# A two-layer diffusion trunk on one core: where the modulation loads and the attention stacks are queued, what landing times the planner assumes, and new strand ranks

## The chip, the cores and the metric

One core of one Trainium2 chip. The metric is the device time of one execution in microseconds, as the median of several runs. Work on the core is done by TensorE (PE, matrix products), VectorE (DVE), ScalarE (ACT), GpSimd (POOL) and by DMA transfers that SyncE (SP), ACT and POOL issue, each in the order of its own queue.

## The reference

Two layers over 512 latent tokens and 256 context tokens, 1024 wide. Cut to what matters:

```python
sh1, sc1, gt1, sh2, sc2, gt2 = split(silu(c) @ w_ada + b_ada, 6)     # latents; the context likewise with c_ctx
h = rmsnorm(x, g1) * (1 + sc1) + sh1
z = h @ w_in                                                       # nine groups of 256 columns
q, k = rope(z[q]), rope(z[k]);  k_all, v_all = context ++ latents
a = softmax(q1 k1) - lam * softmax(q2 k2);  o = a @ v_all          # 4 heads, differential attention
mix = concat(mixer_a(z), mixer_b(z), mixer_c(z), rmsnorm(o))
x = x + gt1 * (mix @ w_out)
h2 = rmsnorm(x, g2) * (1 + sc2) + sh2
x = x + gt2 * ((silu(dwconv3(h2 @ up_a)) * (h2 @ up_b)) @ w_down)   # D_FF = 2816
# the context tokens run through the same weights in layer 0; the second layer needs only their keys and values
return rmsnorm(x, final_g)
```

All is float32. A product is made in three passes: each operand is split into a rounded part (`hi`, `wh`) and the rest (`lo`, `wl`), and PE adds hi*wh, lo*wh and hi*wl.

## The kernel before

The kernel writes no fixed order. It is a set of generators ("strands") that ask for operations, and a planner (`Sched`) that keeps a modelled time for each engine, for each tile's last write and read, and for the DMA system. At each step it advances the strand whose next operation could start first by that model; among those that could start now, the one with the lowest rank (`prio`) goes first. So every constant of the model (`SPC`, the cost of an issue on SP; `LAT`, the latency of a queue) and every rank (`PMC`, `PATT`, `PGM`, `PLATER`, ...) decides in which order instructions are put on the engines' queues. On the chip each queue then runs in that order, and an instruction that waits holds all that stand behind it.

The stages that the steps below speak of:

- **Start.** `start` loads the eight tiles of x, then two "pairs" of modulation weights (`load_pair`, three DMAs of `w_ada0` each, into slots of the pool S), then starts `load_units`, which streams all other weights through SP in the order of `plan`; after three weights it waits until all eight first pairs are issued. `ada_pair` multiplies a pair on PE, transposes the row and adds the bias, which gives one block of shift and scale; `make_h` then makes the block's normed input: `ht` (DVE), `hhi` (ACT), `hlo` (DVE). The first three projections (`batch_t` with q, k and the gate input) go through the eight blocks as these come.
- **Later pairs.** `later` loads and multiplies twelve more pairs, one after the other, for the rest of layer 0's modulation.
- **Stacks.** For attention the rotated q and k are copied to the layout that the score products need: `make_stacks` and `stack` issue 64 SBUF-to-SBUF DMAs per layer, each of 32 partitions, on SP or POOL, as the planner finds earlier.
- **Norm in the middle of a layer.** `final_pass` makes the output projection for one group of tokens after the other and sums squares; `after_mid` makes the normed input `h2`, and stores x to `xacc` in DRAM. The feed-forward products with halves combined (`quads`) need the whole numbers of `h2`: `right_factors` adds `hhi` and `hlo` on POOL (`b`, 8 per layer) and forms the sums `t` from them.
- **Feed-forward.** PE streams w_up and w_dn; ACT rounds each weight (`wh`), DVE or POOL makes the rest (`wl`, `wl_engine`); ACT evicts the down products (`ev`), which POOL's DMAs add to `xacc` in DRAM.
- **Modulation of layer 1.** `next_ada` and `ada_blocks` work through 56 blocks of `w_adaT` (512 KB each) while layer 0's feed-forward and layer 1's beginning run: one DMA on SP, then one or two multiply-and-sum instructions of 128x1024 on DVE, then the bias. They have two buffers of their own. One strand does load and sum in turn.
- **Norm between the layers.** `final_pass` and `after_last` of layer 0 make layer 1's input, and `state["norm"]` is set from the second group on until it is done.

The flag `state["attention"]` limits the engine of `wl` while attention runs: POOL, if its modelled time is less than `WLA` ahead of DVE's.

Of the kernel before, what the change touches and what calls it, by code (L numbers as in the profile page):

```python
# [9 lines left out]
F32 = mybir.dt.float32  # L10
# [70 lines left out]
class Sched:  # L81
# [10 lines left out]
    def __init__(self, nc):  # L92
        self.nc = nc
        self.T = dict(pe=0.0, act=0.0, dve=0.0, pool=0.0, sp=0.0)
        self.dclk = 0.0
        self.port = 0.0
        self.now = 0.0
        self.busy = {}
        self.strands = []
        self.W, self.R = {}, {}  # L100
        self.table = None
        self.full = False
        self.count = 0

# [24 lines left out]
    def _ready(self, req):  # L129
        if callable(req):  # L130
            return req()
        opts, outs, ins, lock = req
        t = [(max(self._deps(o[0], outs, ins) + (PEM if o[0] == "pe" else 0.0), self.T[o[0]],
                  self.port if o[0] in lock else 0.0), o[1]) for o in opts]
        return min(t, key=lambda v: v[0] + v[1])[0] if RDY else min(t)[0]

# [52 lines left out]

    def dma(self, out, in_, queues=("sp",), as_=None):  # L190

        nc = self.nc
        eng = dict(sp=nc.sync, act=nc.scalar, pool=nc.gpsimd)
        cost = dict(sp=SPC, act=0.41, pool=0.55)
        sb = [ap for ap in (out, in_) if ap.space != bass.MemoryType.DRAM]
        outs = [out] if out.space != bass.MemoryType.DRAM else []
        ins = [in_] if in_.space != bass.MemoryType.DRAM else []
        n = 1
        for d in sb[0].shape:
            n *= d  # L200
        t0 = dict(self.T)
        yield from self.op([(q, cost[q], lambda q=q: eng[q].dma_start(*(as_ or (out, in_)))) for q in queues], outs, ins)  # L202
        e = next(q for q in queues if self.T[q] != t0[q])
        self.dclk = max(self.dclk, self.T[e]) + 4 * n / self.BW / 1e3
        t = self.dclk + self.LAT[e]
        for o in outs:
            self._note(self.W, o, t, "dma")
        for i in ins:
            self.R[i.tensor.name].append((*span(i)[1:], t, "dma"))
# [232 lines left out]
def build(tc, a, out):  # L442
    nc = tc.nc
    es = ExitStack()
    with es:
# [9 lines left out]
        K = Sched(nc)  # L455
# [200 lines left out]

        def ada_blocks(l, js, nv, AR, silu, junk):

            for j in js:
                w = yield from AR.get("adaw")  # L660
                yield from K.dma(w, a["w_adaT"][l, j])
                if l and ADAG:
# [27 lines left out]
        def load_pair(b, keep=0):  # L690
            raw = []
            for i in range(3):
                n = 768 if i < 2 else 512
                w = yield from S.get("adaw", keep=keep)
                yield from K.dma(w[:, 0:n], a["w_ada0"][b, i][:, 0:n])
                raw.append(w)
# [163 lines left out]
        def stack(hl, order, r):  # L860
            st = yield from S.get("stk", F32R, keep=KA)
            w = hl[2]
            if STK2:
                for o in range(2):
                    src = hl[o][32 * r:32 * r + 32, 0:w].bitcast(F32)
                    if order[1]:
                        whole, at = st[:, 0:w], st[:, 0:w].rearrange("(a b p) w -> b p a w", a=2, b=2)[o]
                    else:
                        whole = st[64 * o:64 * o + 64, 0:w]
                        at = whole.rearrange("(a p) w -> p a w", a=2)  # L870
                    yield from K.dma(whole.bitcast(F32), src, STKQ, (at.bitcast(F32), src.unsqueeze(1).to_broadcast([32, 2, w])))
                return st
            for i, o in enumerate(order):
# [353 lines left out]
        def start():  # L1227
# [19 lines left out]
            for j in range(2 if START == 0 else 1, 8):  # L1247
                yield from K.when(lambda: j < state.get("blocks", 0) + 5)
                raw0[j] = yield from load_pair(j)
            state["pairs"] = 8  # L1250

        def start_consts():
# [69 lines left out]
        def layer(l):  # L1322
# [44 lines left out]
            K.spawn(bx_copy(pp[2], T, xs, 0), 1)  # L1367
            K.spawn(make_stacks(res, stk), 1)
            if l == 0:
                yield from second_q()  # L1370
                K.spawn(lambdas(), 1)
            if l == 0:
                def later():
                    for i in range(12):
                        raw = yield from load_pair(8 + i, KM)
                        yield from ada_pair(raw, (16 + 2 * i, 17 + 2 * i), 1)
                    yield from make_a(0, 1)
                K.spawn(later(), PLATER)

            def tok_group(g, toks_list, post):  # L1380
# [153 lines left out]
            if not last:  # L1534
                def next_ada():
# [5 lines left out]
                    junk = pool.tile([128, 1024], F32, tag="junk", name="junk")  # L1541
                    AR = Slots(K, pool, [128, 1024], "ar", 2, bufs=2)
                    yield from K.dma(silu, a["cc"], ("pool",))
# [275 lines left out]
QUADS = (0, 1)  # L1819
SPC = 0.36  # L1820
BACT = False
PRF = (1, 1)
MB0 = 3
AVALL = True
SWC = 0.09
RDY = False
PB = 1
LAZY = False
START = 0
STK2 = False  # L1830
EARLY = True
RLQ = ('pool',)
ADAG = 0
PLAIN = (4, 6)
# [5 lines left out]
WLP = 1  # L1840
WLA = 1
WLU = 10
MB = 4
PMC = (1.6, 0.9)
PATT = (1, 0.8)
PATV = (0.9, 1)
PGM = (0.8, 1)
PCMB = (1.1, 1.1)
STKQ = ('sp', 'pool')
KEEP = 1  # L1850
NAQ = 5
KM = 4
KA = 2
NX = 5
PLATER = 1.8
NWR = 4
# [118 lines left out]
```

## Time and profile before

| | us |
|---|---|
| median of 3 runs (1481.15 to 1483.77) | 1482.09 |
| the profiled execution | 1487.35 |
| its span | 1485.5 |
| PE busy in the span | 1425.6 (96%) |
| DVE busy | 1118.8 (75%) |
| ACT busy | 743.2 (50%) |
| POOL busy | 294.0 (20%) |

The span is the time between the first and the last instruction of the profiled execution; 1.9 us of its time lie around it. Busy times are sums over instructions of the profile; PE's granted clock is 0.983 of full speed in the mean.

### The profile page before, as it was taken

Reading aid. Unit: us, or ns where it says so; the run is one execution under the profiler, and the core shown is the slowest. Engines: PE = TensorE matmul, PEld = TensorE weight load, DVE = VectorE, ACT = ScalarE, POOL = GpSimd, SP = SyncE. Lnnn points to the kernel's source line nnn. Section 1 sums busy time; section 2 is a strip of 40 time slices with the busy share of each in tenths; the row PEclk is TensorE's granted clock in tenths of the full one; section 3 lists DMA queues with packets and bytes.
Section 4 is the critical chain, followed back from the end, with each engine's and each line's share of the span. In section 5 each row is a group of like instructions: output and inputs, shape, how many; then the busy total and the mean of one; then the engine's idle time right before and its main releaser. Section 6 shows DMA issues by size and latency. Waiting matters only on the chain.

```text
span 1485.5 us, 23946 instructions
## 1 busy us (share of the span) xinstructions
PE 1425.6 (96%) x9196; PEld 1269.7 (85%) x9196; DVE 1118.8 (75%) x1912; ACT 743.2 (50%) x1185; POOL 294.0 (20%) x320
## 2 busy tenths in 40 slices
PE   6989999999899999999999898999999999999997
PEld 3866888897799999999999886888888889999996
DVE  4727578767788778888777778698878758777875
ACT  5325646524443455545545433465545455665652
POOL 0200232213200021101111110343413011221130
PEclk8989999999999999999999999999999999999998
DMA  9475241324015687667977844524332366677661
GB/s 373 141 236 201 89 132 43 128 86 157 15 59 165 163 210 166 172 169 189 226 191 196 270 170 151 171 100 135 118 108 73 122 134 157 162 181 184 177 191 58
DMA packets 76835, 229.13 MB, mean 154 GB/s; under 512 B 10624, under 2 KB 12800, under 8 KB 76592
## 3 DMA queue, kind: packets, MB, share of 16 engines
q1 hardware_dynamic: 50832, 160.34, 31.7%
q0 software_dynamic: 25600, 66.86, 21.3%
q8 instruction: 72, 1.18, 0.3%
q10 hardware_dynamic: 288, 0.39, 0.1%
q14 instruction: 43, 0.35, 0.1%
HBM read 164.64 MB, written 51.38 MB: 145 GB/s over the span
## 4 chain that ended last, share of the span: by engine, by line
PE 86%; DVE 6%; DMA 4%; SPq 1%; issue 1%; ACT 1%; DVEq 0%; ACTq 0%
PE banks L231 84%; DMA adaw<-in_w_ada 2%; PE banks L244 2%; DMA adaw<-in_w_adaT 1%; SPq L202 1%; DVE wl L283 1%; DVE hlo L299 1%; DVE ht L299 1%; DVE fy L299 0%; ACT hhi L263 0%; DMA mats<-in_mats 0%; DVE by L299 0%; DVE out L299 0%; DVE u L283 0%; DVE ropey L283 0%
## 5 line engine op out<-in xcount | busy, mean ns | idle before, releaser
L273 ACT CAST wh<-wr 128x1024 fp32r<-128x1024 f32 x220 | 229.6, 1048 | 172.1 <-PE banks L231 129.1
L231 PE MATMUL banks<-hlo,wh 128*128 128x512 f32 (+2 forms) x968 | 300.0, 334 | 8.3 <-DVE hlo L299 8.2
L231 PE MATMUL banks<-hhi,wh 128*128 128x512 f32 (+2 forms) x968 | 302.1, 336 | 4.7 <-DVE fy L299 2.1
L231 PE MATMUL banks<-hhi,wl 128*128 128x512 f32 (+2 forms) x968 | 298.6, 333 | 0.4 <-DVE wl L283 0.4
L283 DVE TENSOR_TENSOR wl<-wr,wh 128x1024 fp32r<-128x1024 f32 x196 | 240.2, 1227 | 73.1 <-ACT wh L273 72.6
L213 POOL DMA_DIRECT2D xacc<-ev x128 | 110.8, 866 | 602.7 <-ACT ev L312 590.0
L231 PEld LDWEIGHTS banks<-hlo,wh 128*128 128x128 f32 x968 | 173.5, 190 | 26.9 <-DVE hlo L299 13.9
L231 PEld LDWEIGHTS banks<-hhi,wh 128*128 128x128 f32 x968 | 173.6, 190 | 22.1 <-issue 2.6
L231 PEld LDWEIGHTS banks<-hhi,wl 128*128 128x128 f32 x968 | 173.3, 189 | 14.6 <-DVE wl L283 0.6
L231 PE MATMUL banks<-hi,wh 128*128 128x512 f32 (+1 forms) x560 | 172.0, 349 | 4.2 <-ACT hi L273 4.2
L231 PE MATMUL banks<-lo,wh 128*128 128x512 f32 (+1 forms) x560 | 171.2, 348 | 2.8 <-DVE lo L283 2.6
L231 PE MATMUL banks<-hi,wl 128*128 128x512 f32 (+1 forms) x560 | 170.7, 347 | 0.0
L312 ACT ACTIVATE ev<-banks,ada 128x512 f32<-128x512 f32 x192 | 111.2, 614 | 76.6 <-PE banks L231 51.3
L231 PEld LDWEIGHTS banks<-hi,wh 128*128 128x128 f32 x560 | 96.3, 189 | 18.2 <-ACT hi L273 4.8
L231 PEld LDWEIGHTS banks<-lo,wh 128*128 128x128 f32 x560 | 96.2, 189 | 17.2 <-DVE lo L283 3.5
L231 PEld LDWEIGHTS banks<-hi,wl 128*128 128x128 f32 x560 | 95.9, 189 | 14.3
L283 DVE TENSOR_TENSOR wr<-wr 128x512 f32<-128x512 f32 x136 | 91.0, 687 | 17.3 <-DMA wr<-in_w_up 16.2
L285 POOL TENSOR_TENSOR wl<-wr,wh 128x1024 fp32r<-128x1024 f32 (+1 forms) x24 | 58.8, 2448 | 210.1 <-ACT wh L273 154.7
L231 PE MATMUL banks<-th,wh 128*128 128x384 f32 (+1 forms) x272 | 84.4, 310 | 0.4 <-DVE c L283 0.4
L231 PE MATMUL banks<-th,wl 128*128 128x384 f32 (+1 forms) x272 | 84.5, 311 | 0.0
L231 PE MATMUL banks<-tl,wh 128*128 128x384 f32 (+1 forms) x272 | 84.4, 310 | 0.0
L325 DVE TENSOR_REDUCE mx<-banks 128x1 f32<-128x768 f32 (+1 forms) x80 | 67.7, 847 | 17.8 <-PE banks L231 16.7
(234 smaller groups left out, 2958.2 us busy)
## 6 DMA issues: line engine op xcount, KB each, us to landing
wr<-in_w_up SPq DMA_DIRECT2D x88, 512.0 KB, 4.6
adaw<-in_w_adaT SPq DMA_DIRECT2D x56, 512.0 KB, 5.1
xacc<-ev POOLq DMA_DIRECT2D x64, 384.0 KB, 9.4
wr<-in_w_dn SPq DMA_DIRECT2D x44, 512.0 KB, 5.2
xacc<-ev POOLq DMA_DIRECT2D x64, 256.0 KB, 7.9
adaw<-in_w_ada SPq DMA_DIRECT2D x40, 384.0 KB, 7.1
wr<-in_w_zt SPq DMA_DIRECT2D x24, 512.0 KB, 5.5
wr<-in_w_o SPq DMA_DIRECT2D x16, 512.0 KB, 4.1
```

The source lines that it names most:

```text
L202: yield from self.op([(q, cost[q], lambda q=q: eng[q].dma_start(*(as_ or (out, in_)))) for q in queues], outs, ins)
L213: yield from self.op([("pool", 0.9, lambda: self.nc.gpsimd.dma_start(out, in_, accum_op=ALU.add))], [], [in_])
L231: self.nc.tensor.matmul(o, l, r, start=a, stop=b, skip_group_check=more)
L244: self.nc.tensor.transpose(o, i, ident)
L273: opts.append(("act", 0.19 + n / 1200, lambda: self.nc.scalar.copy(out, in_)))
L283: opts.append(("dve", 0.15 + n / 960, lambda: self.nc.vector.tensor_tensor(out, a, b, op=op)))
L285: opts.append(("pool", 0.1 + n * 2.25e-3, lambda: self.nc.gpsimd.tensor_tensor(out, a, b, op=op)))
L299: lambda: self.nc.vector.scalar_tensor_tensor(out, a, s, b, op0=op0, op1=op1, **k))], outs, ins, lock)
L312: emit = dict(act=lambda: self.nc.scalar.activation(out, a, AF.Copy, scale=s), dve=lambda: self.nc.vector.tensor_scalar(out, a, s, None, o ...
L325: lambda: self.nc.vector.tensor_reduce(out, in_, axis=AX.X, op=op), [out], [in_])
```

## The change

It moves and re-ranks; it changes the computation at one place only (the whole numbers).

- `dma`: an issue on SP costs 0.62 us in the model (`SPC`, before 0.36); a transfer from SP is assumed to land 1 us later (`LSP`), modulation blocks 5 us later (`ADL`), the later pairs 2 us later (`PDL`).
- `ada_blocks`: the loads run in a strand of their own with rank 3.5 and go through POOL's queue (`ADQ`); the sums follow as blocks come. In layer 1 the sums wait until two split weights are ready and no norm is under way (`ADAG`).
- `later`: the loads are a strand of their own (rank 2), one pair ahead; the products have rank 0.5 (before 1.8).
- `stack`: all stack DMAs through POOL (`STKQ`); layer 0's stacks are spawned after the later pairs. An unused branch is dropped.
- `BACT`: the whole numbers are made on ACT (`whole`: `ht` plus the shift, written over x's tile once it is stored), and not as `hhi + hlo` on POOL.
- `START = 2`: after x one pair, then the first three weights, then pairs 1 to 7; a square root on a constant right after the first silu. `LAZY`: the first batch takes its weights as it comes to them.
- `RDY`: a strand's start counts by the engine that would end first. With it on, the new flag `strict` changes nothing.
- New ranks and limits: see the diff.

```diff
-        return min(t, key=lambda v: v[0] + v[1])[0] if RDY else min(t)[0]
+        return min(t, key=lambda v: v[0] + v[1])[0] if RDY or (STRICT and self.strict) else min(t)[0]
...
+        if e == "sp":
+            t += LSP
         for o in outs:
-            self._note(self.W, o, t, "dma")
+            self._note(self.W, o, t + late, "dma")
...
+            def loads():
+                for j in js:
+                    w = yield from AR.get("adaw")
+                    yield from K.dma(w, a["w_adaT"][l, j], ADQ, late=ADL)
+                    ready.append(w)
+            K.spawn(loads(), PAL)
             for j in js:
-                w = yield from AR.get("adaw")
-                yield from K.dma(w, a["w_adaT"][l, j])
+                yield from K.when(lambda: ready)
+                w = ready.pop(0)
...
-                yield from K.dma(w[:, 0:n], a["w_ada0"][b, i][:, 0:n])
+                yield from K.dma(w[:, 0:n], a["w_ada0"][b, i][:, 0:n], late=PDL if b >= 8 else 0.0)
...
-            K.spawn(make_stacks(res, stk), 1)
+            if l:
+                K.spawn(make_stacks(res, stk), 1)
...
+                def later_loads():
+                    for i in range(12):
+                        yield from K.when(lambda: len(ahead) < NPF)
+                        raw = yield from load_pair(8 + i, KM)
+                        ahead.append(raw)
+                K.spawn(later_loads(), PLOAD)
                 def later():
                     for i in range(12):
-                        raw = yield from load_pair(8 + i, KM)
+                        yield from K.when(lambda: ahead)
+                        raw = ahead.pop(0)
                         yield from ada_pair(raw, (16 + 2 * i, 17 + 2 * i), 1)
                     yield from make_a(0, 1)
                 K.spawn(later(), PLATER)
+                K.spawn(make_stacks(res, stk), 1)
...
-SPC = 0.36
-BACT = False
-PRF = (1, 1)
+SPC = 0.62
+LSP = 1.0
+ADL = 5.0
+ADQ = ('pool',)
+NAR = 2
+PDL = 2.0
+NPF = 1
+PLOAD = 2
+STRICT = True
+PAL = 3.5
+BACT = True
+PRF = (1.5, 2.5)
...
-RDY = False
-PB = 1
-LAZY = False
-START = 0
-STK2 = False
+RDY = True
+PB = 0.9
+LAZY = True
+START = 2
...
-ADAG = 0
+ADAG = 2
...
-WLA = 1
+WLA = 2
...
-PMC = (1.6, 0.9)
-PATT = (1, 0.8)
-PATV = (0.9, 1)
-PGM = (0.8, 1)
-PCMB = (1.1, 1.1)
-STKQ = ('sp', 'pool')
+PMC = (1, 1.6)
+PATT = (1, 1)
+PATV = (0.9, 0.9)
+PGM = (1, 1)
+PCMB = (1.1, 1)
+STKQ = ('pool',)
...
-NAQ = 5
-KM = 4
-KA = 2
+NAQ = 6
+KM = 3
+KA = 4
...
-PLATER = 1.8
+PLATER = 0.5
```

## Rows read from the trace of the kernel before

**Rows 1.** The page's 40 slices of the span: PE's busy tenths

```profile
PE   6989999999899999999999898999999999999997
```

**Rows 2.** Stretches (us): length, busy us (xcount) by engine, granted clock, DMA share, GB/s

```profile
0.00:31.00 31.00, 18.53 (x217) 10.07 (x218) 11.28 (x25) 17.18 (x26) 1.58 (x6) 0.87 0.96 369
31.00:80.00 49.00, 49.00 (x336) 41.19 (x335) 34.60 (x73) 19.65 (x31) 10.17 (x17) 0.98 0.56 179
80.00:95.00 15.00, 8.16 (x42) 5.47 (x41) 0.34 (x2) 0.37 (x1) 0.00 (x0) 0.66 0.95 332
361.00:382.00 21.00, 17.14 (x73) 12.04 (x72) 14.91 (x15) 5.56 (x8) 13.51 (x6) 1.00 0.08 32
382.00:396.00 14.00, 11.90 (x64) 9.72 (x62) 10.40 (x13) 9.09 (x10) 3.88 (x2) 1.00 0.09 30
842.00:862.00 20.00, 14.36 (x55) 11.66 (x54) 9.59 (x15) 4.37 (x6) 0.00 (x0) 0.83 0.49 183
885.00:925.00 40.00, 35.06 (x174) 27.78 (x172) 34.06 (x67) 15.49 (x27) 4.93 (x10) 0.91 0.53 185
945.00:965.00 20.00, 16.57 (x121) 15.84 (x120) 11.38 (x24) 11.12 (x18) 4.97 (x2) 0.91 0.47 160
925.00:1110.00 185.00, 179.24 (x1195) 154.93 (x1196) 146.52 (x263) 102.83 (x180) 67.56 (x64) 0.98 0.39 125
400.00:830.00 430.00, 429.27 (x2457) 407.03 (x2456) 350.68 (x553) 212.53 (x312) 56.38 (x66) 1.00 0.66 172
```

**Rows 3.** PE in order of time; idle before it and what ended that in brackets

```profile
23.75 2.90 PE L231 MATMUL banks<-adaw,sl 128*32 128x256 f32 x16 [2.94 <-DMA adaw<-in_w_ada]
...
30.56 0.99 PE L231 MATMUL banks<-hhi,wh 128*128 128x512 f32 x2
...
84.61 1.08 PE L231 MATMUL banks<-adaw,sl 128*32 128x256 f32 x6 [4.48 <-DMA adaw<-in_w_ada]
```

**Rows 4.** SP's queue in order of time

```profile
11.21 2.29 SPq L202 DMA_DIRECT2D wr<-in_w_zt  x3
14.16 17.89 SPq L202 DMA_DIRECT2D adaw<-in_w_ada  x18
...
65.33 0.59 SPq L202 DMA_DIRECT2D stk<-rhi  x1
...
78.60 2.50 SPq L202 DMA_DIRECT2D stk<-rlo  x4
81.22 1.83 SPq L202 DMA_DIRECT2D adaw<-in_w_ada  x3
```

**Rows 5.** The tile stk: issues, count, ns min/median/max, first and last start

```profile
L202 SPq DMA_DIRECT2D stk<-rlo x45: 507/591/1822, 66.6 to 1017.4; - x45
L202 POOL DMA_DIRECT2D stk<-rhi x28: 496/496/586, 65.6 to 1010.7; - x28
```

**Rows 6.** DVE, then POOL, in order of time from 362 us

```profile
362.56 0.75 DVE L299 SCALAR_TENSOR_TENSOR hlo<-ht,ada,hhi 128x512 fp32r<-128x512 f32 x1 [0.79 <-ACT hhi L263]
...
364.77 1.46 DVE L299 SCALAR_TENSOR_TENSOR hlo<-ht,ada,hhi 128x512 fp32r<-128x512 f32 x1 [0.79 <-ACT hhi L263]
...
363.47 2.21 POOL L285 TENSOR_TENSOR b<-hhi,hlo 128x768 f32<-128x768 f32 x1 [7.83 <-DVE hlo L299]
```

**Rows 7.** DVE in order of time, at the sum of one modulation block

```profile
846.42 1.23 DVE L299 SCALAR_TENSOR_TENSOR adaw<-adaw,silu 128x1024 f32<-128x1024 f32 x1 [4.34 <-DMA adaw<-in_w_adaT]
```

**Rows 8.** The tile adaw in two stretches: DVE's busy us and count follow PE's, PEld's

```profile
850.00:900.00 50.00, 0.00 (x0) 0.00 (x0) 8.59 (x14) 0.93 0.57 200
900.00:950.00 50.00, 0.00 (x0) 0.00 (x0) 6.15 (x10) 0.93 0.45 128
```

**Rows 9.** The page's DMA issues: count, KB each, median us to landing

```profile
adaw<-in_w_adaT SPq DMA_DIRECT2D x56, 512.0 KB, 5.1
x<-in_xT POOLq DMA_DIRECT2D x8, 384.0 KB, 7.0
```

**Rows 10.** Waits of all engines: total us, times, longest

```profile
POOL xacc L213 <- ACT ev L312: 590.0, 121, 76.7
```

More of the change, by code (lines that the diff above doesn't have):

```diff
@@ L102, in __init__ @@
         self.full = False
+        self.strict = True
         self.count = 0
@@ L188, in op, with dma @@
             self._note(self.W, o, end, e)
-    def dma(self, out, in_, queues=("sp",), as_=None):
+    def dma(self, out, in_, queues=("sp",), late=0.0):
         nc = self.nc
@@ L201, in dma @@
         t0 = dict(self.T)
-        yield from self.op([(q, cost[q], lambda q=q: eng[q].dma_start(*(as_ or (out, in_)))) for q in queues], outs, ins)
+        yield from self.op([(q, cost[q], lambda q=q: eng[q].dma_start(out, in_)) for q in queues], outs, ins)
         e = next(q for q in queues if self.T[q] != t0[q])
@@ L657, in ada_blocks @@
         def ada_blocks(l, js, nv, AR, silu, junk):
+            ready = []
+            def loads():
[4 more added lines that the diff above has]
+            K.spawn(loads(), PAL)
             for j in js:
-                w = yield from AR.get("adaw")
-                yield from K.dma(w, a["w_adaT"][l, j])
+                yield from K.when(lambda: ready)
+                w = ready.pop(0)
                 if l and ADAG:
@@ L862, in stack @@
             w = hl[2]
[L863 to L872, printed above, removed]
             for i, o in enumerate(order):
@@ L1250, in start @@
             state["pairs"] = 8
+            K.strict = False
         def start_consts():
@@ L1372, in layer @@
             if l == 0:
+                ahead = []
+                def later_loads():
[4 more added lines that the diff above has]
+                K.spawn(later_loads(), PLOAD)
                 def later():
                     for i in range(12):
-                        raw = yield from load_pair(8 + i, KM)
+                        yield from K.when(lambda: ahead)
+                        raw = ahead.pop(0)
                         yield from ada_pair(raw, (16 + 2 * i, 17 + 2 * i), 1)
@@ L1541, in next_ada @@
                     junk = pool.tile([128, 1024], F32, tag="junk", name="junk")
-                    AR = Slots(K, pool, [128, 1024], "ar", 2, bufs=2)
+                    AR = Slots(K, pool, [128, 1024], "ar", NAR, bufs=NAR)
                     yield from K.dma(silu, a["cc"], ("pool",))
```

## Prediction

> **What bounds the kernel now.** I read the page's slices first [rows 1]: PE is busy nearly throughout, so the time can only fall where PE stands still or runs at the lower of its two clock levels (1.2 instead of 2.4 GHz). Next I cut the span into stretches [rows 2]. From 400 to 830 us PE is busy for 429.27 of 430 us at clock 1.00: layer 0's feed-forward is bound by PE, and no order of the same products makes it shorter. The loss is in a few places between. For each I take two numbers from its row: idle time (length less PE's busy time), and clock loss, (1 less the granted clock) times the length, since at half clock half of the time is lost. The second also counts what falls on idle time, so a sum of both is an upper bound.
>
> - 0 to 31 us: idle 12.5. PE's first projection product starts at 30.56 [rows 3], and DMA is busy for 0.96 of the stretch. From 31 to 80 PE has no gap.
> - 80 to 95: idle 6.84, clock 5.1; together 11.9.
> - 361 to 396 (norm in layer 0): idle 3.86 + 2.10 = 6.0, clock none.
> - 842 to 862: idle 5.64, clock 3.4; together 9.0.
> - 885 to 925 (norm between the layers): idle 4.94, clock 3.6; together 8.5.
> - 945 to 965: idle 3.43, clock 1.8; together 5.2.
>
> The last five make 40.6 us. Start and end aside, little else is lost. The question is how much of this the change removes and what it puts in its place.
>
> **Start.** Order on SP now: x, pair 0, pair 1, three weights (issued at 11.21), pairs 2 to 7 from 14.16 [rows 4]. The change puts the weights ahead of pair 1. DMA moves 369 GB/s here [rows 2], so the pair of 1.05 MB that is overtaken is 2.8 us: the first weights come 2.8 us earlier, pair 1 later by the 1.5 MB of three weights, 4.3 us. The norm's input for block 0 can be ready as early as before, and PE no longer multiplies pairs 2 and 3 ahead of it, which it does from 23.75 on [rows 3]. The later pairs come when they came before, at one per 2.8 us, while PE needs longer per block than that: from 31 to 80 it has no gap although the pairs come in between. So PE starts the projections up to 7 us earlier (30.56 - 23.75 = 6.8), but waits for the second and third pair meanwhile. Gain 0 to 7, I take 3, which is about the 2.8 us of one pair. The early square root only moves a table load from before the norm's root to before the squares: 0.
>
> **Stacks out of SP's queue, pairs loaded ahead.** At 65.33 SP begins to issue stacks, at 78.60 the last four, and only at 81.22 pair 8, for which PE waits from 80 on [rows 3, 4]: 16 us of issues at 0.59 each [rows 5], and waits for the rotated k, stand ahead of loads that need nothing. DMA is at 179 GB/s from 31 to 80, half of what it gives at the start [rows 2]: there is room. With the stacks on POOL, and pair loads as a strand that asks for the next pair before the last is multiplied, pair 8 can land before 80. Of 11.9 us I take 9 (4 to 12); the wait that remains is for the following pairs, which come one behind the other.
> What this costs on POOL: SP's 81 issues (45 + 36) move there, at 0.50 each [rows 5], 40 us over two layers. The first two heads of a t need 32 issues, 16 us alone on POOL, against the 16 us that both queues took from 65 to 81. So the stacks are ready at about the same time, and what is queued behind them on POOL (the rest of some weights, `wl`) waits as long as it did. Cost 0; the upper end, all 16 us on the path in both layers, needs PE to have nothing else, and PE is busy then. I leave 0 to 6.
>
> **A rule against it.** The rows show POOL's stack issues at 496 ns in the median and 586 at most, while DVE is at work beside them for 35 of 49 us [rows 2, 5]. The Trainium skill, page "SBUF — State Buffer", section "SBUF: two separate sides", says that a DMA from GpSimd's queue cannot get its descriptors written while VectorE runs a copy in its two-port mode; the section "A bandwidth-pool intuition that's wrong" gives some 620 ns alone and 3100 overlapped. By that, 32 stacks would take 99 us instead of 16 and attention would begin far too late. The trace does not agree for these issues (586 ns at most). Since 137 issues move to that queue, the rule raises the chance of the third rival below from 0.11 to 0.14.
>
> **Whole numbers on ACT.** In the norm of layer 0, `hlo` on DVE takes 0.75 us alone and 1.46 while POOL adds `b` beside it for 2.21 us [rows 6]; six of eight `hlo` are like that (1.46 or 1.47). So 6 x 0.71 = 4.3 us of DVE go, and a similar 2 to 3 us at the sums behind (DVE busy 10.40 of 14 us, with the last two `b` in it). POOL loses the 8 adds, 8 x 2.2 = 18 us. PE's loss there is 6.0; I take 5 (3 to 6). ACT gains 16 instructions of at most the 0.7 us of `hhi` in layer 0; it is busy for 5.56 of 21 us [rows 2], so they hide. The added wait: `whole` writes over x and so waits for x's store to DRAM; behind it on ACT stands the next `hhi`. The store needs only x, so it is early. Cost 0 (to 2). In layer 1 the same adds stand where PE has no loss: 0.
>
> **Modulation blocks of layer 1.** At 846.42 DVE takes up a block's sum after 4.34 us of waiting for its DMA [rows 7]; behind it stand `wl` and the feed-forward's last gating, and PE starves. I ascribe a part of the loss in the two later stretches to the same cause. The change lets the load be issued a block ahead, assumes landing 5 us later, and forbids the sums in the norm between the layers, where DVE is busy for 34.06 of 40 us. From POOL a load is slower: 7.0 us to landing for 384 KB against 5.1 for 512 KB from SP [rows 9], about the 2 us that the 5 us cover. The issues are 56 x 0.5 = 28 us of POOL, spread over 600 us. I take 6 of 9.0 us (0 to 9) at 842, 4 of 8.5 (-3 to 8.5) at 885, 3 of 5.2 (-2 to 5) at 945.
> What is put off: between 850 and 950 stand 24 instructions, 12 sums [rows 8], 12 x 1.3 = 16 us of DVE. Those in the norm go behind it, to 925 to 1110, where DVE is busy for 146.5 of 185 us: 38 us are free, but attention's chain runs through DVE. Cost 2 (0 to 9).
>
> **The rest: ranks, slot limits, the planner's figures.** They reorder everything, and no row shows the new order. A new order has waits of its own: nearest are the five stretches above, of 5 to 12 us each. I take one small one, 5 us (-5 to 15; below nothing, since an issue on SP costs 0.59 in the rows and 0.36 in the old model, so the new order is planned with truer figures).
>
> **Sum.** Gains 3 + 9 + 5 + 6 + 4 + 3 = 30, costs 0 + 0 + 2 + 5 = 7, net 23 us. The profiled execution, 1487.35 us with a span of 1485.5, would become 1464; it lies 5.3 us above the median of the runs. From the median: 1482.1 - 23 = **1459 us**. All upper gains and no costs: 47.5 + 5, so 1430. All lower gains (2) and all costs (32): 1512.
>
> **Rivals.**
> *1. Only the start and layer 0 gain.* The blocks' sums still stand in DVE's queue at places where their load, now behind accumulates on POOL, isn't there; the three stretches after 842 stay as they are. Then 3 + 9 + 5 = 17 less 7: 1472. For it: POOL's accumulates wait for ACT 121 times, 590 us in all [rows 10], and the loads stand in that queue. Against it: 5 us more are assumed.
> *2. It does not do what it says.* The strands ask for the same things at nearly the same planned times: with two buffers and a load that waits for none, the second block could be loaded ahead before as well, and `strict` is without effect. Stalls move by a few us: 1482.
> *3. Slower: GpSimd's queue.* A load of a block stands behind an accumulate, which waits for ACT 4.9 us in the mean (590/121) and up to 76.7. If the load then comes later than the 5 us, DVE waits as at 846 and PE loses 9 us each time. Now PE loses nothing between 400 and 830, and DVE is busy for 350.7 of 430 us there, so a wait of a few us is not made up at once. The gains outside (3 + 9 + 5) less 7 make 10; it decides from the second such stall on. With four: 36 - 10 = 26 slower, 1508; with three, 1499. I put it at 1500.
>
> **How the numbers follow.** A difference under 0.2% (3 us) can't be told from none here. Chances: forecast (1440 to 1476) 0.60, rival 1 (1470 to 1479) 0.18, rival 2 (1479 to 1485) 0.08, rival 3 0.14. Faster 0.78, same 0.08, slower 0.14. The range leaves one in ten out at each end: 1436 lies near the sum of the upper gains with half of the cost, 1490 takes in the near part of rival 3.
>
> **What would show it.** Right: no idle PE near 80 us and a granted clock of 1.00 there; `hlo` at 0.75 us throughout the norm; no wait of DVE for `adaw` over 1 us, and PE at clock 1.00 from 830 to 965. The start is right if the first projection product comes near 25 us. Wrong: waits of DVE for `adaw` between 450 and 830, gaps of PE in that stretch, stack issues on POOL far above 0.5 us, or new gaps of PE in attention, from 925 to 1110 or from 100 to 350, where `mx` waits for stacks.

## The result, and the profile after

| | before | changed |
|---|---|---|
| time, us (median, fastest to slowest) | 1482.05 (1481.15 to 1483.77) | 1463.53 (1461.79 to 1466.38) |
| profiled execution, us | 1487.35 | 1462.63 |
| its span, us | 1485.5 | 1460.9 |
| granted clock, mean | 0.983 | 0.990 |

The changed kernel is faster by 1.3%: ratio 0.9872, with an interval from 0.9856 to 0.9887. The prediction, 1459 us, lies 4.5 us below it. By the medians the gain is 18.5 us, by the two spans 24.6 us. Of the 6.1 us between the two, 5.3 are what the profiled execution of before lay above its median, and 0.9 what that of the changed kernel lay below its own, so every distance between these two traces below is too kind to the change by up to that much. Between two kernels I compare medians, and traces only for the place of a gain.

The page of the changed kernel: engines, then PE's busy tenths in 40 slices and its granted clock in tenths.

```profile
PE 1414.9 (97%) x9196; PEld 1265.8 (87%) x9196; DVE 1119.2 (77%) x1899; ACT 754.5 (52%) x1216; POOL 369.7 (25%) x456
...
PE   6999999999999999999999999998999999999997
PEclk9999999999999999999999999999999999999998
```

In [rows 1] PE had eights in slices 2, 10, 22 and 24 (counted from 0); here one is left, slice 27 (986 to 1023 us), in layer 1's attention. Stretches of the changed kernel, placed by the work in them; the columns are those of [rows 2] (length, then busy us and count of PE, PEld, DVE, ACT and POOL, granted clock, DMA share, GB/s).

```profile
78.00:91.00 13.00, 10.72 (x91) 7.98 (x91) 1.37 (x5) 1.33 (x3) 6.89 (x14) 1.00 1.05 281
352.00:373.00 21.00, 20.55 (x90) 15.24 (x89) 13.57 (x20) 14.90 (x20) 0.00 (x0) 1.00 0.08 31
373.00:388.00 15.00, 15.00 (x88) 13.19 (x87) 14.86 (x20) 9.40 (x13) 7.88 (x4) 1.00 0.11 37
820.00:845.00 25.00, 24.00 (x115) 20.47 (x114) 18.12 (x27) 7.92 (x11) 5.41 (x10) 1.00 0.70 253
845.00:860.00 15.00, 15.00 (x104) 13.37 (x103) 9.36 (x14) 7.32 (x12) 1.88 (x3) 1.00 0.11 36
860.00:900.00 40.00, 40.00 (x250) 35.29 (x250) 36.37 (x63) 20.14 (x33) 10.26 (x13) 1.00 0.41 145
900.00:1095.00 195.00, 181.89 (x1208) 155.17 (x1207) 164.39 (x285) 111.54 (x201) 96.25 (x118) 0.98 0.43 133
```

Four of the five stretches of [rows 2] in which PE stood still or ran at half its clock are nearly closed: 2.3 us idle near 80 (6.84 before) at clock 1.00 (0.66 before); 0.45 in layer 0's norm (6.0); 1.0 from 820 to 900 at clock 1.00 throughout (10.6 from 842 to 862 and 885 to 925 together, at 0.83 and 0.91). The last line is the other side: in layer 1's attention, where the fifth (945 to 965) lay, PE idles for 13.1 us, 5.8 before, and DVE is busy for 164 of 195 us.

Landmarks of PE's order, changed less before, in us, show the same as a running sum:

| landmark | before | changed | difference |
|---|---|---|---|
| first projection product | 30.6 | 27.0 | -3.6 |
| layer 0, last output projection | 351.6 | 341.8 | -9.8 |
| layer 0, first combined feed-forward product (`th`, the rounded part of the sums `t`) | 431.4 | 414.9 | -16.4 |
| layer 0, last `th` product | 845.0 | 827.8 | -17.3 |
| layer 1, first projection | 889.4 | 865.0 | -24.4 |
| layer 1, first scores | 943.0 | 909.8 | -33.1 |
| layer 1, last output projection | 1116.2 | 1087.6 | -28.7 |
| last product | 1478.1 | 1453.7 | -24.3 |

At layer 1's first scores the change is 33 us ahead, and then gives 9 back: 4.4 in the attention, 4.4 behind it, where the granted clock was 0.95 (1088 to 1162) and 0.94 (1420 to 1450) and had been 1.00 before.

### The profile page after: what moved, and what is told of

Read it like the earlier page. It is cut to its first block, busy times and chain, and to the rows that moved or that the text cites. A ratio compares the mean times of both kernels' runs of the same rounds, so it can differ in the third digit from the quotient of the medians.

```text
span 1460.9 us, 23874 instructions
## 1 busy us (share of the span) xinstructions
PE 1414.9 (97%) x9196; PEld 1265.8 (87%) x9196; DVE 1119.2 (77%) x1899; ACT 754.5 (52%) x1216; POOL 369.7 (25%) x456
## 3 DMA queue, kind: packets, MB, share of 16 engines
q1 hardware_dynamic: 36576, 121.67, 24.6%
## 4 chain that ended last, share of the span: by engine, by line
PE 83%; DVE 7%; DMA 4%; issue 3%; POOL 1%; ACT 1%; SPq 0%; DVEq 0%; POOLq 0%; ACTq 0%
PE banks L234 82%; DMA adaw<-in_w_ada 2%; PE banks L247 2%; DVE mx L328 1%; DVE wl L286 1%; DMA stk<-rhi 1%; DMA x<-in_xT 0%; DVE shuf L286 0%; DMA wr<-in_w_dn 0%; DVE ropey L286 0%; POOL p L317 0%; DVE p L302 0%; POOL avr L1056 0%; DVE mlo L286 0%; DVE by L302 0%
## 5 line engine op out<-in xcount | busy, mean ns | idle before, releaser
L286 DVE TENSOR_TENSOR wl<-wr,wh 128x1024 fp32r<-128x1024 f32 x189 | 230.5, 1222 | 74.2 <-ACT wh L276 61.6
L288 POOL TENSOR_TENSOR wl<-wr,wh 128x1024 fp32r<-128x1024 f32 (+1 forms) x31 | 77.4, 2504 | 117.0 <-ACT wh L276 89.6
L203 POOL DMA_DIRECT2D adaw<-in_w_adaT x56 | 34.2, 623 | 220.2 <-DVE adaw L302 158.7
```

The costliest lines, as they stand in the source:

```text
L286: opts.append(("dve", 0.15 + n / 960, lambda: self.nc.vector.tensor_tensor(out, a, b, op=op)))
L288: opts.append(("pool", 0.1 + n * 2.25e-3, lambda: self.nc.gpsimd.tensor_tensor(out, a, b, op=op)))
```

## Experiments

Two kinds were run. In a *frozen* build the planner still reckons with the old queue or engine, so the order on every engine is that of its parent, and only the emission of some instructions differs. In a *planned again* build a constant differs, and the order follows. Times are medians of three rounds; the difference is to the changed kernel's 1463.53 us if nothing else is said. Before ran beside them at 1482.7 to 1483.0, within 1 us of its 1482.05. An interval of a ratio is some 0.3% to either side, 4 us, so a difference under 4 us (2, 5, 6, 10) isn't sure from the times alone, and one of 5 or 6 (1, 4) hardly is; there the traces have to bear it out.

### 1. Stacks back on SP's queue, order frozen

```diff
 yield from K.dma(st[32 * i:32 * i + 32, 0:w]..., hl[o][32 * r:32 * r + 32, 0:w]...,
-                 STKQ)
+                 STKQ, real="sp")   # the planner counts POOL, SP issues it
```

> The changed kernel's own plan, with the order on PE, DVE and ACT untouched; only the 128 stack DMAs are issued on SP instead of POOL, at the places where the plan has them. Theory (stacks in SP's queue hold the loads behind them): PE waits for a later pair near 80 us again and falls to the lower clock there; 7 to 12 us slower than the changed kernel, 1470 to 1476. Rival (it was the strand that asks for pairs ahead, the queue is indifferent): no gap over 3 us near 80, 1462 to 1467.

1469.56 us, +6.0; ratio 0.991, 0.9879 to 0.9941, to before. The wait for the pairs near 80 is back. PE's waits from 60 to 135 us of this build, then of the changed kernel (total us, times, longest):

```profile
PE banks L234 <- DMA adaw<-in_w_ada: 5.8, 4, 4.4
```

```profile
PE banks L234 <- DMA adaw<-in_w_ada: 2.2, 3, 1.8
```

The granted clock from 91 to 105 us is 0.88, in the changed kernel 1.00. By layer 0's last scores 5.7 us are lost, and after that nothing more (4.8 at the end). So in this order the stack queue is worth 6 us, all of it near 80 us, as the prediction's step said; it took 9 for that queue and the earlier pair loads together.

### 2. Modulation loads back on SP, order frozen

```diff
-yield from K.dma(w, a["w_adaT"][l, j], ADQ, late=ADL)
+yield from K.dma(w, a["w_adaT"][l, j], ADQ, late=ADL, real="sp")
```

> The changed kernel's own plan, with the order on PE, DVE and ACT untouched; only the 56 loads of layer 1's modulation blocks are issued on SP instead of POOL. Theory (the assumed landing and the load ahead did it, the queue does not matter): within 3 us of the changed kernel, 1461 to 1467, no wait of DVE for adaw over 1 us. Rival (on SP the loads stand behind weights that wait for a buffer): waits of DVE for adaw come back, 8 us or more slower, 1472 and up.

1464.91 us (ratio 0.9875, 0.9851 to 0.9899): the same. A load takes 5.5 us from issue to landing here and 6.5 from POOL, and neither is waited for. So GpSimd's queue neither brings nor costs anything that shows for these 56 loads.

### 3. Whole numbers back on POOL, in ACT's places

```diff
-yield from K.act(b[:, c], t[:, c], AF.Identity, bias=gt(l, 3, j, g[2]))
+# planned as on ACT, emitted as
+nc.gpsimd.tensor_tensor(b[:, c], hi[:, c], lo[:, c], op=ALU.add)
```

> The changed kernel's own plan, with the order on PE and DVE untouched; only the whole numbers are made as hhi + hlo on POOL, at the places where ACT made them. Theory (POOL's additions slow DVE's hlo, and PE follows DVE in that norm): hlo 1.46 us again, 4 to 7 us slower, 1467 to 1471, all of it before the first combined feed-forward product of layer 0. Rival (PE has enough to do there, the gain in this stretch came from the order): under 2 us, 1462 to 1466.

1481.65 us; ratio 0.9991, 0.9978 to 1.0005, to before: the whole gain is gone, three times what the contention was to cost. The trace shows another mechanism. POOL in order of time, then one line of ACT from 388 us (start, length, what it does, idle before it and its releaser), and the stretch 385 to 400:

```profile
358.80 1.51 POOL L1525 TENSOR_TENSOR x<-hhi,hlo 128x512 f32<-128x512 f32 x1 [1.89 <-DMA xacc<-x]
360.26 0.56 POOL L203 DMA_DIRECT2D xacc<-x  x1
362.72 1.50 POOL L1525 TENSOR_TENSOR x<-hhi,hlo 128x512 f32<-128x512 f32 x1 [1.90 <-DMA xacc<-x]
...
383.33 0.57 POOL L203 DMA_DIRECT2D silu<-in_cc  x1
...
388.50 1.91 ACT L266 ACTIVATE silu<-silu 128x2048 f32<-128x2048 f32 x1 [15.57 <-DMA silu<-in_cc]
...
385.00:400.00 15.00, 6.67 (x20) 5.38 (x21) 9.42 (x13) 9.78 (x11) 7.21 (x4) 0.54 0.41 155
```

An addition overwrites x (the whole numbers' tile) and waits for x's store; the next store is issued by POOL itself, behind that addition. So one store's landing after the other (1.9 us each) stands in POOL's order between the eight additions, and the `silu` load, next in POOL's order, is issued at 383.33 instead of 344.89. ACT waits for it, the feed-forward's first gating waits for ACT, PE stands still for 10.1 us, and the granted clock of the stretch is 0.54. This build therefore doesn't measure contention.

### 4. The additions back on POOL as extra work

The changed kernel with its eight `whole` on ACT, and POOL additions of the same size put back *behind* the loads; DVE's sums wait for them.

```diff
 b1, b2 = wholes[2 * q][0], wholes[2 * q + 1][0]
+# once for each of the eight blocks, behind POOL's loads:
+nc.gpsimd.tensor_tensor(b[:, 0:T], hi[:, 0:T], lo[:, 0:T], op=ALU.add)
```

> The changed kernel with its order on PE, DVE, ACT and SP untouched, and POOL's additions hhi + hlo put back on top, behind the loads that POOL issues there: they write the same whole numbers once more, and the sums t on DVE wait for them. Theory (POOL's additions slow DVE and DVE's sums wait for them, as before the change): hlo 1.46 us again, 4 to 7 us slower than the changed kernel, 1467 to 1471. Rival (the gain of that stretch came from the new order around it, the additions cost little): under 2 us, 1462 to 1466. The run with the additions in ACT's places gave 18 us, of which only a part can be this; the rest would be POOL's queue, where each addition waited for x's store and the load for ACT's silu stood behind.

1468.79 us, +5.3 (ratio 0.9892, 0.9863 to 0.992, to before). DVE in layer 0's norm, in this build and then in the changed kernel:

```profile
355.36 1.47 DVE L302 SCALAR_TENSOR_TENSOR hlo<-ht,ada,hhi 128x512 fp32r<-128x512 f32 x1 [0.79 <-ACT hhi L266]
...
358.29 1.47 DVE L302 SCALAR_TENSOR_TENSOR hlo<-ht,ada,hhi 128x512 fp32r<-128x512 f32 x1 [0.79 <-ACT hhi L266]
```

```profile
354.96 0.75 DVE L302 SCALAR_TENSOR_TENSOR hlo<-ht,ada,hhi 128x512 fp32r<-128x512 f32 x1 [0.79 <-ACT hhi L266]
...
357.17 0.75 DVE L302 SCALAR_TENSOR_TENSOR hlo<-ht,ada,hhi 128x512 fp32r<-128x512 f32 x1 [0.79 <-ACT hhi L266]
```

From one block's `hlo` to the next it takes 2.93 us with the addition beside it and 2.21 without. PE waits for `hlo` 8 times, 4.3 us in all, from 340 to 420 us, against 0.3 us. That is the [rows 6] effect by itself, and its size.

### 5. The old first loads, planned again

```diff
-START = 2
-LAZY = True
+START = 0
+LAZY = False
```

> The changed kernel, planned anew with the first loads as before (x, two pairs, three weights) and the first batch taking its three weights at once. Theory (the 3.6 us gained at the first projection product stay until the end): first projection product near 30.6 us, 3 to 4 us slower, 1466 to 1468. Rival (a later wait takes them up): under 1.5 us, 1462 to 1465.

1464.71 us, +1.2 (ratio 0.9878, 0.9849 to 0.9908, to before). PE's first projection product is at 30.6 us again, 3.6 later, yet at layer 0's last scores 2.3 us of that are left and at the last product 1.3. Where the head start goes is not in one place, and +1.2 us is within the doubt, so no gain that lasts is shown.

### 6. The old figures of the planner

```diff
-SPC = 0.62; LSP = 1.0; ADL = 5.0; PDL = 2.0
+SPC = 0.36; LSP = 0.0; ADL = 0.0; PDL = 0.0
```

> The changed kernel planned anew with the old figures: 0.36 us for an issue on SP, no later landings (SPC, LSP, ADL, PDL). Theory (the assumed landings removed the waits of VectorE for the blocks and of PE for the pairs): waits of DVE for adaw come back, 6 to 13 us slower, 1469 to 1477. Rival (loading ahead is enough, the figures only shift the order): within 3 us, 1461 to 1467.

1467.16 us, +3.6 (ratio 0.9884, 0.985 to 0.9917, to before). Both kinds of wait that the theory named come back. DVE's waits for modulation blocks in this build, from 385 to 820 us (total us, times, longest; in the changed kernel one of 0.8 us):

```profile
DVE adaw L302 <- DMA adaw<-in_w_adaT: 14.3, 11, 2.0
DVE junk L302 <- DMA adaw<-in_w_adaT: 7.1, 4, 3.6
```

They cost PE nothing: in that stretch it is busy for all 435 us. PE's own waits for the pairs, from 60 to 260 us, are 4.7 us instead of 2.2, and by layer 0's last scores 3.2 us are lost, as many as at the last product. So the theory had the waits right and their price, 6 to 13 us, wrong, because PE has no wait at all from 385 to 820. What the assumed landings do in the norm between the layers this build can't show: with the old figures the planner puts all 56 blocks' sums ahead of 792 us.

### 7. The old ranks and limits

```diff
-PMC = (1, 1.6); PATT = (1, 1); PATV = (0.9, 0.9); PGM = (1, 1); PCMB = (1.1, 1)
-NAQ = 6; KM = 3; KA = 4; PLATER = 0.5; PRF = (1.5, 2.5); WLA = 2; PB = 0.9
+PMC = (1.6, 0.9); PATT = (1, 0.8); PATV = (0.9, 1); PGM = (0.8, 1); PCMB = (1.1, 1.1)
+NAQ = 5; KM = 4; KA = 2; PLATER = 1.8; PRF = (1, 1); WLA = 1; PB = 1
```

> The changed kernel planned again with the old ranks and limits (those of the products, the attention's parts, the held-back weights, the slots of the stacks and pairs). The prediction gave the ranks and the new order together 5 us, bounds of -5 to 15. Theory (they are worth about that): 1466 to 1472 us. Rival (the queues and the whole numbers alone carry the change and the ranks are worth nothing): 1461 to 1465 us.

1473.08 us, +9.5 (ratio 0.9934, 0.9911 to 0.9958, to before), 1 us above the theory's range, which is within the doubt. From layer 0's last output projection to its first `th` product it needs 80.6 us instead of 73.1, with one wait for the gating (`fy`) that names the place, and ahead of it on DVE three sums `t` like the second line, beside three remainders of POOL:

```profile
382.63 0.58 PE L234 MATMUL banks<-hhi,wh 128*128 128x256 f32 x1 [5.33 <-DVE fy L302]
...
376.20 2.78 DVE L302 SCALAR_TENSOR_TENSOR t<-t,x 128x384 f32<-128x384 f32 x1
...
373.33 7.91 POOL L288 TENSOR_TENSOR wl<-wr,wh 128x1024 fp32r<-128x1024 f32 x3 [0.77 <-ACT wh L276]
```

The three sums take 2.64 to 2.78 us each, and 0.55 where POOL is idle. That is the contention of [rows 6] again, from other work of POOL: with the whole numbers on ACT, the gain of this stretch also needs an order that keeps POOL's remainders off the sums ahead of the gating.

### 8. The sums not held out of the norm, planned again

```diff
-ADAG = 2
+ADAG = 0
```

> The changed kernel planned anew with layer 1's sums allowed at any time (ADAG 0). Theory (keeping them out of the norm between the layers is worth the idle and slow PE from 885 to 925): PE idle and at the lower clock again around 870 to 900, 3 to 8 us slower, 1466 to 1472. Rival (the sums put off cost as much in attention as they cost in the norm): within 2 us, or faster, 1459 to 1466.

**1452.44 us**, 11.1 less than the changed kernel; ratio 0.9787, 0.9754 to 0.9821, to before. This beats both kernels. PE's order is that of the changed kernel up to 855 us, in the norm between the layers, so the difference arises behind that: at layer 1's first scores this build is 0.4 us later than the changed kernel, at layer 1's last output projection 8.3 us earlier. This build, from 845 us on:

```profile
845.00:900.00 55.00, 55.00 (x344) 47.82 (x343) 49.42 (x91) 27.82 (x45) 14.52 (x22) 1.00 0.46 154
900.00:950.00 50.00, 49.67 (x389) 46.41 (x388) 39.21 (x69) 32.34 (x52) 26.36 (x37) 1.00 0.47 132
950.00:1000.00 50.00, 49.26 (x271) 38.87 (x270) 45.63 (x86) 31.40 (x52) 32.97 (x40) 1.00 0.45 127
1000.00:1050.00 50.00, 47.47 (x304) 37.87 (x303) 41.27 (x69) 28.08 (x56) 18.68 (x14) 1.00 0.30 102
```

The changed kernel in the same stretches:

```profile
845.00:900.00 55.00, 55.00 (x352) 48.66 (x351) 45.73 (x76) 27.46 (x45) 12.13 (x15) 1.00 0.33 116
900.00:950.00 50.00, 46.72 (x363) 43.26 (x362) 38.86 (x70) 30.15 (x50) 28.18 (x41) 1.00 0.56 164
950.00:1000.00 50.00, 45.25 (x239) 35.36 (x238) 45.12 (x67) 24.94 (x42) 35.35 (x43) 1.00 0.46 135
1000.00:1050.00 50.00, 47.33 (x286) 37.37 (x286) 43.44 (x81) 33.35 (x66) 24.04 (x19) 0.97 0.31 109
```

In the first line PE is busy for all 55 us in both: holding the sums out of the norm frees DVE there (45.73 instead of 49.42 us) and buys PE nothing. In the three lines behind it the changed kernel's PE has 139.3 us and the other's 146.4.

### 9. The held sums cut short, order frozen

What is it that costs, DVE's time for the held sums or the order around them? The last ten sums take 8 of 1024 columns, so ten modulation values lack most of their sum; waits and order stay.

```diff
 yield from K.stt(w if v == nv - 1 else junk, w, 1.0, silu[:, v, :], ALU.mult, ALU.mult, accum=d,
+                 cut=8 if l and j >= 38 else None)
```

> The changed kernel's own order on every engine; VectorE's last ten block sums of layer 1's modulation (the ones that the change puts off into layer 1's attention) take 8 of 1024 columns each, so ten modulation values are wrong, and about 10 x 1.1 = 11 us of VectorE's work in 860 to 1045 us is gone, while the waits for the blocks' transfers stay. Theory (the put-off sums cost by the VectorE time that they take from the attention, which is what the build without the putting-off gave back): the time falls by 7 to 11 us, to 1453 to 1457 us. Rival (what costs is the order that the planner writes around the put-off sums, with its stack slots and products, not the 11 us of VectorE): it falls by 0 to 3 us, 1460 to 1464 us, and layer 1's last score product stays within 3 us of 1032 us.

1456.71 us, 6.8 less than the changed kernel (ratio 0.9822, 0.9796 to 0.9848, to before), at the lower edge of the theory; layer 1's last score product comes at 1025.7 us instead of 1032.1. The changed kernel's sums and then this build's in the tile adaw (count, ns min/median/max, first and last start), from 800 and from 900 us on:

```profile
L302 DVE SCALAR_TENSOR_TENSOR adaw<-adaw,silu x14: 1212/1218/1221, 800.1 to 1042.2; 128x1024 f32<-128x1024 f32 x14
```

```profile
L302 DVE SCALAR_TENSOR_TENSOR adaw<-adaw,silu x9: 152/161/163, 903.8 to 1035.8; 128x8 f32<-128x8 f32 x9
```

Nine sums stood in the attention; 9 x (1.218 - 0.161) = 9.5 us of DVE went, and 6.8 us of the time. From 1000 to 1050 the granted clock is 1.00 again (0.97). So in this order most of what the sums cost is the time that they take from DVE. How they come to cost it, on DVE in the changed kernel:

```profile
979.37 2.99 DVE L286 TENSOR_TENSOR ada<-ada,vec 128x1 f32<-128x1 f32 x1
982.28 1.21 DVE L302 SCALAR_TENSOR_TENSOR adaw<-adaw,silu 128x1024 f32<-128x1024 f32 x1
...
984.76 0.95 DVE L328 TENSOR_REDUCE mx<-banks 128x1 f32<-128x768 f32 x1
```

The bias addition of an earlier block and two sums (982.28 and 983.62) stand ahead of a maximum of scores, and the chain of work that ended last runs through all of them. The addition takes 2.99 us instead of 0.15, beside a remainder of POOL from 979.93 to 982.33. It stays in the build with cut sums (2.98 us), so the 6.8 us don't hold all that the putting off costs. What is left of the 11 us of experiment 8, some 4 us, is within the doubt on the two times; how far this addition makes it up, and how far the order, is not shown.

### 10. Held for one split weight rather than two

```diff
-ADAG = 2
+ADAG = 1
```

> The changed kernel planned again with the sums held only until one split weight stands ready, rather than two (and still not in the norm). Up to layer 1's norm its order is the changed kernel's. Theory (the time lost in layer 1's attention grows with how long the sums are held): between the two builds, 1454 to 1461 us. Rival (it is the bar on the norm, which this build keeps, or the luck of one order): 1462 to 1466 us, as the changed kernel.

1465.70 us (ratio 0.9881, 0.9852 to 0.9909): the same as the changed kernel, as the rival said. Only four sums stand behind 900 us here, not nine, and still nothing is won: layer 1 from its first scores to its last output projection takes 184.8 us (changed kernel 177.8 with nine; no holding 169.1 with three; the old figures of experiment 6 178.5 with none). PE's waits from 840 to 1100 us, of this build:

```profile
PE banks L234 <- ACT p L266: 4.2, 1, 4.2
PE banks L247 <- DVE p L302: 3.5, 3, 2.4
PE banks L234 <- DMA stk<-rhi: 2.6, 1, 2.6
```

So a plan for this stretch can also lose 7 to 15 us in other ways. The number of sums there doesn't order the four builds, and experiment 8 is not proof that holding must cost 11 us in every order. Only experiment 9 prices the sums alone, and for one order.

### 11 and 12. The kernel before, with its stacks on POOL, order frozen

```diff
 # 11: all 128 issues of the stacks on POOL
-                 STKQ)
+                 STKQ, real="pool")
 # 12: those of layer 0 alone
+                 STKQ, real="pool" if len(nstk) <= 16 else None)
```

> The kernel before with its own plan, the order on PE, DVE and ACT untouched; only the 81 stack DMAs that it issues on SP are issued on POOL. Theory (the stacks in SP's queue were what held pair 8): no idle PE near 80 us, 5 to 10 us faster than before, 1472 to 1477. Rival (without the strand that asks ahead the loads come no earlier): within 2 us of before, 1480 to 1484.

> The kernel before in its own order on every engine, with the stack transfers of layer 0 alone issued by GpSimd; those of layer 1 stay on the two queues as before. Theory (in layer 0 the move is worth the 6 to 7 us that the build with all of them moved had gained by layer 0's output projection; its later loss came from the stacks of layer 1, which stand in GpSimd's order ahead of its remainders and collide with VectorE): 1474 to 1477 us, with the last product 5 to 8 us earlier than before. Rival (the gain of layer 0 is given back later whatever layer 1's stacks do): 1480 to 1484 us.

All stacks moved: 1492.87 us, slower than before (ratio 1.0062, 1.004 to 1.0085). Only layer 0's: 1481.81 us, no change (0.9998, 0.9979 to 1.0016). In both the wait of 4.48 us at 84.61 [rows 3] is gone, and PE waits for the pairs behind it instead: 3.5 us in all with all stacks moved, from 60 to 130 us, 8.7 before, and for layer 0's stacks alone:

```profile
PE banks L231 <- DMA adaw<-in_w_ada: 5.9, 3, 3.1
```

My theory of 6 to 7 us for layer 0 falls by the medians. That trace's last product is 7.2 us earlier than that of before, but the trace of before lies 5.3 above its median; it is the medians that I go by.

With all stacks moved, layer 1's attention took 184.2 us, against 173.3 before and 172.7 with layer 0's alone. POOL and then DVE of that build there:

```profile
947.62 0.50 POOL L202 DMA_DIRECT2D stk<-rlo  x1
948.13 2.40 POOL L285 TENSOR_TENSOR wl<-wr,wh 128x1024 fp32r<-128x1024 f32 x1
955.33 2.39 POOL L285 TENSOR_TENSOR wl<-wr,wh 128x1024 fp32r<-128x1024 f32 x1 [4.80 <-ACT wh L273]
...
948.42 2.93 DVE L299 SCALAR_TENSOR_TENSOR p<-p,c 128x768 f32<-128x768 f32 x1
...
955.95 2.84 DVE L299 SCALAR_TENSOR_TENSOR adaw<-adaw,silu 128x1024 f32<-128x1024 f32 x1 [3.28 <-DMA adaw<-in_w_adaT]
...
959.78 1.01 DVE L299 SCALAR_TENSOR_TENSOR p<-p,c 128x768 f32<-128x768 f32 x1
```

POOL's remainder `wl` stands behind the 32 stacks, several of which wait, and so runs beside DVE's `p` (the attention weights), which takes 2.93 us instead of 1.01; the second `wl` falls on a block sum, 2.84 us instead of the 1.22 of its kind [rows 7]. The next `p` stands behind that sum, and PE waits 5.6 us for it. That is one of the waits of this stretch, followed to its end; that it makes up all the 11 us I haven't shown.

## Why the prediction was right, and where it was not

The forecast held in direction and roughly in size: 23 us predicted, 18.5 measured. Its steps did less well, and that the sum came out close is in part luck: the put-off sums cost more than was taken (6.8 to 11.1 us for 2), while the stretches after 842 gave more (16 for 13) and the 5 us set down for ranks and figures were no cost. The stated range, 1436 to 1490, takes in no change at all (1482), so that the time fell into it says little.

| step | predicted, us | measured, us | from |
|---|---|---|---|
| start | gain 3 (0 to 7) | 3.6 at the first product, 1.2 at the end | 5 |
| stacks and pair loads | gain 9 (4 to 12) | 6.0 for the stack queue | 1 |
| whole numbers | gain 5 (3 to 6) | 5.3 | 4 |
| modulation blocks at 842, 885, 945 | gain 13 (-5 to 22) | 16 up to the first scores, by landmarks | below |
| sums put off | cost 2 (0 to 9) | 6.8 for DVE's time; 11.1 with the order | 8, 9 |
| stacks on POOL's queue | cost 0 (0 to 6) | PE waits 2.5 for a stack | trace |
| ranks and figures | cost 5 (-5 to 15) | undone: ranks +9.5, figures +3.6 | 6, 7 |

**What held.** *The limits of the stretches*: the time came out of four of the five places that idle time and clock had marked, and 400 to 820 stayed at PE's own speed (435 us of 435 from 385 to 820). *The stacks*: right, a little under. *The whole numbers*: right in mechanism and size, `hlo` at 0.75 us throughout; only that the order has to keep POOL's remainders off the same sums (experiment 7). *Rival 3* didn't come: DVE's waits for modulation loads from 385 to 860 us are 0.8 us in all. *The rule weighed in the prediction* (the Trainium skill, page "SBUF — State Buffer", sections "SBUF: two separate sides" and "A bandwidth-pool intuition that's wrong") doesn't show in these 128 issues either:

```profile
L203 POOL DMA_DIRECT2D stk<-rhi x64: 498/498/585, 63.6 to 996.3; - x64
L203 POOL DMA_DIRECT2D stk<-rlo x64: 498/498/507, 64.9 to 1000.6; - x64
```

Beside VectorE at 37 of 51 us (27 to 78) and 164 of 195 us the slowest takes 585 ns; a stretched one of 3100 ns doesn't occur. But the rule speaks of copies of VectorE in its two-port mode, and of VectorE's operations beside these issues none is a copy from SBUF to SBUF: its copies there read PSUM (`banks`). So the case that the rule speaks of did not arise among these issues, and they speak neither for it nor against it; the prediction counted the 586 ns against it without asking for that. *The signs*: the first projection product comes at 27.0 us, not near 25, and new gaps of PE in layer 1's attention, set down as a sign of being wrong, did come.

**The sums put off: the mis-sized term.** The prediction set 16 us of DVE's work (14.7 by the busy times of [rows 8]) against 38 us of DVE's idle time in the attention and took 2, with 9 as the upper end. Nine sums cost 6.8 by their time on DVE alone (9.5 us of it), 70 per cent, though DVE was to have a fifth of the stretch free. The sentence "attention's chain runs through DVE" stood there and wasn't followed: the free time lies where DVE waits for a score, and a sum that runs when the score comes delays the maximum, the exponentials and the next product (the lines of experiment 9). The upper end should have been the whole 16 us.

**The transition: right place, one remedy without effect, the others not told apart.** The prediction gave the gains after 842 to three remedies: loads issued a block ahead, later landings assumed, sums held out of the norm. How long two sections take, in us (layer 0's last `th` product to its last down-projection product; layer 1's first projection to its first scores):

| kernel | down projection | norm and projections |
|---|---|---|
| before | 44.1 | 53.5 |
| before, stacks on POOL (11) | 44.2 | 53.8 |
| before, layer 0's alone (12) | 42.8 | 52.5 |
| changed | 36.9 | 44.8 |
| loads on SP (2) | 36.9 | 45.4 |
| stacks on SP (1) | 36.9 | 43.7 |
| additions on POOL (3) | 36.9 | 45.6 |
| old first loads (5) | 36.9 | 46.1 |
| old figures (6) | 36.8 | 44.9 |
| old ranks (7) | 36.9 | 45.1 |
| sums not held (8) | 36.9 | 44.0 |

Some 7 and 9 us are gained, and none of the seven parts, each undone alone, gives back more than 1.3 of them. Holding the sums is not what brings it: without it (8) nine sums stand between the last `th` product and the first scores, in the changed kernel three, in the kernel before thirteen. Nor is it the sums' own time: with the old figures (6) none is left there, and the sections are no shorter. What the builds with the new order have in common is that DVE does not wait for a block there; before, it waits 7.9 us in three times from 845 to 943. So the prediction saw DVE's wait of 4.34 us [rows 7] rightly as the place. What took these waits away stays open: the strand that loads the blocks by itself, the planner's rule to weigh what would end first rather than begin first (`RDY`), or the assumed landings. No run undoes the first two, and experiment 6, which undoes the landings, has no blocks left in this stretch.

**The ranks and figures: no price of their own.** They were taken as a cost of 5; undone in the new order, they cost time instead. But the parts don't add. Undone one at a time from the changed kernel, start, stacks, whole numbers, figures and ranks cost 1.2 + 6.0 + 5.3 + 3.6 + 9.5 = 25.6 us, the transition comes to it with 16, the held sums with -11.1: 30.5, not 18.5 (with some 4 us of doubt on each). And the stack queue, worth 6.0 when it is taken out of the new order, brings nothing (12) or costs 10 (11) when it is put into the old one. A sum over parts, as the prediction made it, assumes that each is worth the same in either order; these were not.

## What to carry to other kernels

Before work is moved into a stretch because the engine has idle time there, look at what that engine's idle time waits for: if the bounding engine's chain runs through it, price the moved work in full (here 6.8 us for 9.5), and check first that the stretch that it leaves needs relief (here PE had no gap in either case). A queue or an engine is to be changed together with the plan that reckons with it: one move was worth +6, 0 or -10 us depending on the order around it. On an in-order queue, look at what stands *behind* the moved instruction: the additions on POOL cost 18 us where a load had to wait for them, and 5 where none did.

## What the runs showed of the hardware

- VectorE's operations on SBUF tiles took longer while GpSimd added or subtracted SBUF tiles beside them: `hlo` 1.47 us instead of 0.75, `p` 2.93 instead of 1.01, a block sum 2.84 instead of 1.22, an addition of one column 2.99 instead of 0.15.
- A DMA issue of a stack holds GpSimd for 498 ns and SP for 565 to 588 in the median; that of a modulation block holds GpSimd for 572 ns and SP for 328. A block of 512 KB lands 6.5 us after its issue by GpSimd, 5.5 by SP, and 56 of them took the same time in all by either.
- A stop of PE of 10.1 us goes with a granted clock of 0.54 in the stretch 385 to 400 (experiment 3), so nearly all of it at 1.2 GHz, the lower level; the short waits near 80 us in the changed kernel (2.2 us in three) left it at 1.00.
